# Sixteen more frames by gather in a hybrid encoder block with product-key experts

## The chip, the cores and the metric

The kernel runs on one NeuronCore of a Trainium2 chip. The metric is device time in microseconds of one execution. TensorE multiplies (its stationary operand is loaded by a separate instruction), VectorE and ScalarE do elementwise work, GpSimd (POOL) builds tiles and issues indirect transfers, SyncE (SP) issues plain ones; 16 DMA engines move the data.

## The reference

One layer over 512 frames of width 2048, in float32, and a final norm:

```
xn = rmsnorm(x);  p_rw, q, c_kv, iq, ik, iw, gates = split(xn @ w_in)
y_a = rwkv7(p_rw) @ w_branch_rwkv            # 16 heads of 64, a recurrence over time
y_b = dsa(q, c_kv, iq, ik, iw) @ w_branch_dsa # 16 heads; iq, ik, iw choose 256 keys per frame
h = x + (sig(gA) * y_a + sig(gB) * y_b) @ w_out
h2 = rmsnorm(h)
# product-key experts: 8 heads choose 16 of 16384 experts each, 128 per frame
out = h + sum_k gate_k * gelu(h2 . u[e_k]) * v[e_k]
return rmsnorm(out)
```

u and v are tables of 16384 rows of 2048 floats, 128 MB each.

## The kernel before

Every float32 matrix is split into a rounded high part and a remainder (`load_w`, L187; `split`, L224), and a product is three matmuls: high by high, high by low, low by high. `load_w` moves 512 KB into one of three `raw` buffers on SP's queue; ScalarE copies it to `whi` (L196), VectorE subtracts to `wlo` (L197), two buffers of each. `load_w` has a raised priority, so that it is placed ahead of about a hundred instructions. A planner orders the instructions of each engine before the run; each engine then works in that order.

Front: `r1` (L379) computes three small projection tiles and, for eight head pairs, three projection tiles and the pair's scaled tensors. `r1_pair` (L440) sums log decays by matmuls with the 256-column constant `u2`, which holds an inclusive and an exclusive lower triangle. `index` (L701) projects the latent keys, the index keys (tile 33, the 64 columns of `ik` twice: L735), the index queries and the queries, and interleaves the triangular `solve` on VectorE. `r2` runs the recurrence in chunks and projects the gates. `attention` (L863) evacuates V as [128, 4, 1024]; `head` (L895) multiplies 64 columns of V by the transposed weights into the upper or lower 64 rows of one PSUM tile (L922). `mix` and `peer` (L928) follow.

Experts: the 512 frames are treated in two ways. The last ND = 352 go through the dense loop, all 16384 experts for every frame, with gates that are zero for experts not chosen. The first NG = 160 gather their own 128 rows of u and of v.

`route` (L1026) computes the choice, writes one-hot gate products to DRAM (`d_g`, 22 groups of 16 frames: L1120 on) and, between, the activations of the first EARLY = 24 blocks of 128 experts (`early`, stored in `d_a`). `experts` (L1156) goes over 16 groups `cg` of eight blocks. For each block it takes the activation (`act`: two loads of 512 KB and 48 matmuls; or a copy from `d_a`), multiplies it by G, the group's gates (one buffer, read from `d_g`), and splits it into Wh and Wl (eight buffers each). Then 16 output blocks `db`: one load of 512 KB and 24 matmuls (L1195 to L1197) each, added to `accT` by VectorE (L1202). The order of groups is 3, 0, 4, 1, 5, 2, 6, ...: groups 0 to 2 are wholly early, the others not.

`gathered` (L988) is a generator of 320 steps, and `step` (L980) takes from it at an even rate as the dense loop proceeds, two units per computed block and one per `db`. A step is an indirect transfer of 128 rows of 8 KB into one of three `rows` buffers (issued by POOL) and one VectorE instruction over 2048 elements: a dot product with `ra`/`rb` (L1002) or an accumulation (L1011). Frames 128 to 159 use four partitions each (32 steps per table), frames 0 to 127 one (128 steps per table). `issue_after` places a step's VectorE instruction behind the last `wlo`.

At the last group the activations' pool is closed, `turned` (L1213) loads the residual and transposes `accT` block by block, and after `db` 11 the rest of the steps and `final_gathered` (L1247) are issued: load h into a buffer `hg` (one, for both blocks of frames), fold the four partitions by matmuls, add, square, norm, store. `final` norms and stores the dense frames.

```
        self.due += n * 320 / (512 - 2 * EARLY - 10)
...
        order = [g for i in range(n) for g in (n + i, i)] + list(range(2 * n, 16))
...
                if last and db == 11:
                    for _ in items:
                        pass
                    self.final_gathered()
```

Of the kernel before, what the change touches and what calls it, by code (L numbers as in the profile page):

```python
# [30 lines left out]
T = 512  # L31
# [6 lines left out]
NTILE = 74  # L38
NG = 160
ND = T - NG  # L40
EARLY = 24

VEC = {}
_o = 0
# [7 lines left out]
for _n, _w in (("ident", 128), ("iota", 128), ("onesbd", 128), ("ones64", 128), ("onesD", 2), ("onesR", 2), ("u2", 256),  # L52
               ("mtt", 128), ("mm1", 128), ("mbr", 64), ("m32", 128), ("c30", 128), ("c38", 128), ("fold", 128)):
    CON[_n] = (_o, _w)
    _o += _w
NCON, NKEEP = _o - 128, 256


def columns():
    r = np.arange  # L60
    none = lambda n: np.full(n, -1)
    tiles = [r(3072, 3200), r(3200, 3328), np.concatenate([r(3328, 3360), r(5216, 5224), none(88)])]
# [4 lines left out]
    tiles += [np.concatenate([r(5152, 5216)] * 2)]  # L67
# [6 lines left out]
def constants():  # L74
    c = np.zeros((128, NCON + 128), np.float32)
# [12 lines left out]
    put("u2", np.concatenate([(hp == hf) & (p <= f), (hp == hf) & (p < f)], 1))  # L88
# [7 lines left out]
    put("fold", p % 32 == f % 32)  # L96
# [69 lines left out]
class Kernel:  # L166
# [105 lines left out]
    def build(self):  # L272
        tc, nc = self.tc, self.nc
        with ExitStack() as es:
# [19 lines left out]
            self.d_iq = d("d_iq", [4, 2, 128, 512])  # L294
            self.d_ya = d("d_ya", [2, 8, 128, 512], F32R)
            self.d_gate = d("d_gate", [16, 128, 2, 512])
            self.d_h = d("d_h", [T, D])
            self.d_g = d("d_g", [ND // 16, 16, 128, 128])
            self.d_a = d("d_a", [EARLY, 128, ND])
# [79 lines left out]
    def r1(self, xs):  # L379

        nc, io = self.nc, self.io
        with ExitStack() as es:
# [10 lines left out]
            with self.pool("r1w") as wp:  # L393
# [20 lines left out]
                nc.scalar.activation(iwT[32:64], ps[32:64], AF.Copy, scale=IDX_SCALE)  # L414
                pw = self.wk()
# [24 lines left out]
    def r1_pair(self, p, z, sp, rp, zwa, wicl, lws):  # L440
# [5 lines left out]
        P, Pm, Pi = t1("P"), t1("Pm"), t1("Pi")  # L446
        for b in range(2):
            pc = self.wk()
            for u in range(2):
                nc.tensor.matmul(pc[:, 256 * u:256 * u + 256], lws[:, 2 * b + u, fs], self.c("u2"), start=True, stop=True)  # L450
            g = pc.rearrange("p (u e t) -> p u e t", u=2, e=2)
            o = lambda a: a[:, 256 * b:256 * b + 256].rearrange("p (u t) -> p u t", u=2)
            nc.scalar.activation(o(P), g[:, :, 0], AF.Exp, scale=-CDEC)
            nc.scalar.activation(o(Pm), g[:, :, 1], AF.Exp, scale=-CDEC)
            nc.scalar.activation(o(Pi), g[:, :, 0], AF.Exp, scale=CDEC)
# [16 lines left out]
        v.tensor_tensor(sp[:, 0], kk, Pm, op=ALU.mult)  # L472
# [56 lines left out]
    def r2(self, xs):  # L529
# [3 lines left out]
        with ExitStack() as es:  # L533
# [8 lines left out]
            for p in range(8):  # L542
# [14 lines left out]
                for m in (2 * p, 2 * p + 1):  # L557
                    for j in range(2):
                        ps = self.mm()
                        self.gemm(ps, io["w_in"][42 + 2 * m + j], xs)  # L560
# [140 lines left out]
    def index(self, xs, steps):  # L701
# [7 lines left out]
        with ExitStack() as es:  # L709
# [41 lines left out]
            for h in range(8):  # L751
                ps = self.mm()
                gemm(ps, io["w_in"][34 + h])
# [109 lines left out]
    def attention(self, es, ybh, ybl):  # L863
# [5 lines left out]
        V = kp.tile([128, 4, 1024], F32, name="Vh")  # L869
        for sb in range(4):  # L870
            for hf in range(2):
# [4 lines left out]
                sc.activation(V[:, sb, f], ps, AF.Copy)  # L876
# [18 lines left out]
    def head(self, h, qb, ap, B, qs, ks, V, ybh, ybl):  # L895
# [3 lines left out]
        s = slice(64 * (h % 2), 64 * (h % 2) + 64)  # L899
# [28 lines left out]
    def peer(self):  # L928
# [3 lines left out]
        with ExitStack() as es:  # L932
# [3 lines left out]
            self.ra = gk.tile([128, D], F32, tag="ra", name="ra")  # L936
            self.rb = gk.tile([128, D], F32, tag="rb", name="rb")
            for n, w, dt in (("eid", 128, I32), ("act", 128, F32), ("gate", 128, F32)):
                setattr(self, n + "a", gk.tile([128, w], dt, name=n + "a"))
                setattr(self, n + "b", gk.tile([128, w // 4], dt, name=n + "b"))  # L940
# [4 lines left out]
            with self.pool("hn") as np_:  # L945
# [18 lines left out]
                nc.gpsimd.tensor_tensor(self.rb[0:32], hn[0:32, 1], gf[0:32], op=ALU.mult)  # L964
                for j in range(1, 4):
                    nc.gpsimd.dma_start(self.rb[32 * j:32 * j + 32], self.rb[0:32])
                nc.gpsimd.tensor_tensor(self.ra, hn[:, 0], gf, op=ALU.mult)
# [12 lines left out]
    def step(self, items, n=1):  # L980

        self.due += n * 320 / (512 - 2 * EARLY - 10)
# [5 lines left out]
    def gathered(self):  # L988

        nc, io = self.nc, self.io  # L990
        v = nc.vector

        def rows(table, eid, s):
            r = self.rows.tile([128, D], F32, name="rows")
# [3 lines left out]
        for x, n in (("b", 32), ("a", 128)):  # L998
            h, eid, act, gate = [getattr(self, m + x) for m in ("r", "eid", "act", "gate")]
# [4 lines left out]
            nc.scalar.activation(act, act, AF.Gelu)  # L1004
            v.tensor_tensor(act, act, gate, op=ALU.mult)
            o = self.gk.tile([128, D], F32, tag="r" + x, name="o" + x)
            setattr(self, "r" + x, o)
            for s in range(n):
# [5 lines left out]
                yield  # L1014

# [10 lines left out]
    def route(self, es, xs):  # L1026
# [8 lines left out]
        eid1 = kp.tile([32, 128], I32, name="eid1")  # L1035
# [3 lines left out]
        with ExitStack() as es3:  # L1039
# [3 lines left out]
            for h in range(8):  # L1043
# [48 lines left out]
                for e, b in ((self.eida, 0), (eid1, 1)):  # L1092
# [201 lines left out]
```

## Time and profile before

| | us |
|---|---|
| runs shown | 4137.31, 4136.78, 4130.66 (median 4136.78) |
| profiled execution | 4133.32, span 4131.5 |
| TensorE busy | 3993.7 |
| VectorE busy | 2810.0 |
| ScalarE busy | 1413.8 |
| POOL busy | 797.0 |

The profile is of one execution, so sums are made against 4133.32. Engine names in rows: PE is TensorE (PEld its weight loads), DVE VectorE, ACT ScalarE, POOL GpSimd, SPq SyncE's queue. A busy TensorE is not one at its peak: the durations of its instructions overlap, so paces are read from starts. A row of a stretch has its bounds, its length, the busy time of PE, PEld, DVE, ACT and POOL (with their instructions), the granted clock as a share of 2.4 GHz, the DMA engines' busy share and GB/s. A row of a group has its instructions' busy time and the mean ns of one.

### The profile page before, as it was taken

The page shows a single profiled execution, that of the slowest core. Times are in us where ns is not written, and L with a number is a line of the kernel's source. Part 1 is how long each engine was busy: PE and PEld are TensorE (multiplying, and loading weights), DVE is VectorE, ACT ScalarE, POOL GpSimd, SP SyncE. Part 2 cuts the span into 40 slices and gives each one's busy share as a digit, 9 for nine tenths or more (in the row PEclk, how much of TensorE's full clock was granted, in tenths as well). Part 3 has the DMA queues.
Part 4 walks back from the last instruction along what each step waited for, and adds up shares of the span by engine and source line. Part 5 has one row for each costly group of instructions (what it writes and reads, how often), then busy time and mean ns, then how long its engine had stood idle before and what let it go on. Part 6 is the DMA issues. An engine that isn't in the chain of part 4 may idle for free.

```text
span 4131.5 us, 57533 instructions
## 1 busy us (share of the span) xinstructions
PE 3993.7 (97%) x22313; PEld 3599.7 (87%) x22313; DVE 2810.0 (68%) x4713; ACT 1413.8 (34%) x2079; POOL 797.0 (19%) x919
## 2 busy tenths in 40 slices
PE   8999999999999999999999999999999999999996
PEld 6777778888886788788899998989999999999996
DVE  5444589434434552389976778878888888888886
ACT  4222332223224422332486333323333333333332
POOL 2000211101003300100364222221222221222220
PEclk9999999999999999999999999999999999999998
DMA  4333852332226433333476888988989989999885
GB/s 147 121 127 128 186 177 85 99 101 91 86 93 192 141 133 138 128 130 110 158 214 207 332 318 323 332 323 325 335 332 344 337 328 332 343 342 340 330 332 175
DMA packets 254657, 910.36 MB, mean 220 GB/s; under 512 B 26912, under 2 KB 78240, under 8 KB 210384
## 3 DMA queue, kind: packets, MB, share of 16 engines
q1 hardware_dynamic: 132800, 447.21, 31.4%
q0 software_dynamic: 76176, 436.41, 29.6%
q10 hardware_dynamic: 45408, 23.07, 2.0%
q8 instruction: 175, 2.87, 0.3%
q14 instruction: 98, 0.80, 0.1%
HBM read 830.07 MB, written 75.66 MB: 219 GB/s over the span
## 4 chain that ended last, share of the span: by engine, by line
PE 57%; issue 12%; DMA 5%; POOL 3%; DVE 3%; ACT 2%; POOLq 0%; DVEq 0%; ACTq 0%; SPq 0%
PE mm L213 9%; PE mm L214 9%; PE mm L212 9%; PE wk L1197 5%; PE wk L1196 5%; PE wk L1195 5%; POOL rows L995 3%; PE wk L856 1%; PE wk L855 1%; PE wk L857 1%; PE po L212 1%; PE po L213 1%; DMA G<-d_g 1%; PE po L214 1%; PE po L922 1%
## 5 line engine op out<-in xcount | busy, mean ns | idle before, releaser
L196 ACT ACTIVATE whi<-raw 128x1024 fp32r<-128x1024 f32 x760 | 804.1, 1059 | 1955.9 <-PE mm L213 1018.1
L197 DVE TENSOR_TENSOR wlo<-raw,whi 128x1024 fp32r<-128x1024 f32 x760 | 934.1, 1230 | 773.5 <-ACT whi L196 710.4
L1197 PE MATMUL wk<-Wh,wlo 128*128 128x352 f32 x2048 | 668.5, 327 | 17.4 <-DVE wlo L197 17.3
L1195 PE MATMUL wk<-Wh,whi 128*128 128x352 f32 x2048 | 666.0, 327 | 15.2 <-ACT Wh L225 11.4
L1196 PE MATMUL wk<-Wl,whi 128*128 128x352 f32 x2048 | 669.0, 327 | 0.3 <-DVE Wl L226 0.2
L212 PE MATMUL mm<-h2h,whi 128*128 128x352 f32 (+1 forms) x1920 | 641.0, 334 | 5.2 <-ACT whi L196 5.0
L214 PE MATMUL mm<-h2h,wlo 128*128 128x352 f32 (+1 forms) x1920 | 640.8, 334 | 0.6 <-DVE wlo L197 0.6
L213 PE MATMUL mm<-h2l,whi 128*128 128x352 f32 (+1 forms) x1920 | 639.9, 333 | 0.0
L212 PE MATMUL mm<-xh,whi 128*128 128x512 f32 x1184 | 479.6, 405 | 6.6 <-DVE lo L715 5.1
L213 PE MATMUL mm<-xl,whi 128*128 128x512 f32 x1184 | 476.5, 403 | 0.6 <-POOL xl L344 0.5
L214 PE MATMUL mm<-xh,wlo 128*128 128x512 f32 x1184 | 474.0, 400 | 2.0 <-DVE wlo L197 2.0
L1197 PEld LDWEIGHTS wk<-Wh,wlo 128*128 128x128 f32 x2048 | 388.6, 190 | 25.4 <-DVE wlo L197 24.8
L1195 PEld LDWEIGHTS wk<-Wh,whi 128*128 128x128 f32 x2048 | 387.9, 190 | 22.0 <-ACT Wh L225 13.6
L1196 PEld LDWEIGHTS wk<-Wl,whi 128*128 128x128 f32 x2048 | 388.1, 190 | 3.9 <-DVE Wl L226 3.1
L212 PEld LDWEIGHTS mm<-h2h,whi 128*128 128x128 f32 x1920 | 362.3, 189 | 16.6 <-ACT whi L196 5.3
L214 PEld LDWEIGHTS mm<-h2h,wlo 128*128 128x128 f32 x1920 | 361.4, 188 | 13.0 <-DVE wlo L197 2.1
L213 PEld LDWEIGHTS mm<-h2l,whi 128*128 128x128 f32 x1920 | 363.2, 189 | 10.5
L1011 DVE SCALAR_TENSOR_TENSOR oa<-rows,acta,oa 128x2048 f32<-128x2048 f32 x127 | 297.8, 2345 | 3.0 <-DMA rows<-in_rv_dram,eida 2.9
L1002 DVE CUSTOM_DVE_ANT_0 rows<-rows,ra 128x2048 f32<-128x2048 f32 x128 | 292.1, 2284 | 2.9 <-DMA rows<-in_ru_dram,eida 2.9
L212 PEld LDWEIGHTS mm<-xh,whi 128*128 128x128 f32 x1184 | 224.6, 190 | 60.6 <-DVE lo L715 5.3
L213 PEld LDWEIGHTS mm<-xl,whi 128*128 128x128 f32 x1184 | 224.7, 190 | 56.4 <-issue 3.8
L214 PEld LDWEIGHTS mm<-xh,wlo 128*128 128x128 f32 x1184 | 224.3, 189 | 56.6 <-DVE wlo L197 2.4
(437 smaller groups left out, 5809.9 us busy)
## 6 DMA issues: line engine op xcount, KB each, us to landing
raw<-in_pu_dram SPq DMA_DIRECT2D x256, 512.0 KB, 5.9
raw<-in_pv_dram SPq DMA_DIRECT2D x256, 512.0 KB, 7.3
raw<-in_w_in_dram SPq DMA_DIRECT2D x148, 512.0 KB, 3.8
d_g<-Gs ACTq DMA_DIRECT2D x22, 1024.0 KB, 6.2
G<-d_g POOLq DMA_DIRECT2D x16, 1408.0 KB, 14.1
raw<-in_wbr_dram SPq DMA_DIRECT2D x32, 512.0 KB, 4.0
raw<-in_wout_dram SPq DMA_DIRECT2D x32, 512.0 KB, 3.5
raw<-in_wpq_dram SPq DMA_DIRECT2D x32, 512.0 KB, 3.6
```

The source lines that it names most:

```text
L196: nc.scalar.activation(hi, raw, AF.Copy)
L197: self.last = nc.vector.tensor_tensor(lo, raw, hi.bitcast(F32), op=ALU.subtract).ins
L212: nc.tensor.matmul(ps, hi[:, s], xh, start=k == 0, stop=False)
L213: nc.tensor.matmul(ps, hi[:, s], xl, start=False, stop=False)
L214: nc.tensor.matmul(ps, lo[:, s], xh, start=False, stop=k == nk - 1)
L855: mmul(ps[tb], yh[:, k, t], hi[:, s], start=k == 0, stop=False)
L995: nc.gpsimd.indirect_dma_start(out=r, out_offset=None, in_=table, in_offset=bass.IndirectOffsetOnAxis(ap=eid[:, s:s + 1], axis=0))
L1002: v.tensor_tensor_reduce(r, r, h, 1.0, 0.0, op0=ALU.mult, op1=ALU.add, accum_out=act[:, s:s + 1])
L1011: v.scalar_tensor_tensor(o, r, act[:, s:s + 1], o, op0=ALU.mult, op1=ALU.add)
L1195: mmul(ps, hi[:, s], wh, start=j == 0, stop=False)
L1196: mmul(ps, hi[:, s], wl, start=False, stop=False)
L1197: mmul(ps, lo[:, s], wh, start=False, stop=j == 7)
```

## The change

NG goes from 160 to 176, ND from 352 to 336. The gathered frames are three groups: 16 frames with eight partitions each (16 steps per table), 32 with four, 128 with one: 176 steps per table. Their normed inputs go to DRAM (`d_h2`) and are read back per group. Each group ends with its own fold, residual, norm and store inside `gathered`, in buffers of the `rows` ring, at four steps per group; `final_gathered` is gone, and the steps that remain are issued before the last group's output blocks.

24 early blocks remain, but two in each even group of eight and one in each odd one; the groups run in order 0 to 15. The rate of steps is now 364 over 256 + 2 x 104 - 20 units.

Two joined changes: `u2` holds the inclusive triangle alone, in 128 columns, and the exclusive factor is the inclusive one shifted by a column, with the first column of each 64-frame chunk copied; and V is kept as [64 columns, 64 zeros, 64 columns] per pair of heads, so that both heads of a pair accumulate over all 128 rows of the same PSUM tile.

The index keys' 64 columns move into the unused columns of projection tile 2; the split is stored to DRAM (`d_ik`) and read back in `index`. Tile 33 is gone.

```diff
-NTILE = 74
-NG = 160
+NTILE = 73
+NG = 176
-EARLY = 24
+GROUPS = ((160, 16, 8), (128, 32, 4), (0, 128, 1))
+EARLY = [8 * g + j for g in range(16) for j in range(2 - g % 2)]
...
+                ik = [wp.tile([128, T], F32R, name=f"ik{i}") for i in range(2)]
+                nc.scalar.activation(ik[0][64:128], ps[64:128], AF.Copy)
+                nc.vector.tensor_tensor(ik[1][64:128], ps[64:128], ik[0][64:128].bitcast(F32), op=ALU.subtract)
+                for i in range(2):
+                    nc.gpsimd.dma_start(self.d_ik[i], ik[i][64:128].bitcast(F32))
...
-                nc.tensor.matmul(pc[:, 256 * u:256 * u + 256], lws[:, 2 * b + u, fs], self.c("u2"), start=True, stop=True)
+            nc.tensor.matmul(pc[:, 128 * b:128 * b + 128], lws[:, b, fs], self.c("u2"), start=True, stop=True)
...
-        v.tensor_tensor(sp[:, 0], kk, Pm, op=ALU.mult)
+        v.tensor_tensor(sp[:, 0, 1:], kk[:, 1:], P[:, 0:T - 1], op=ALU.mult)
+        v.tensor_copy(sp[:, 0, 0:T:64], kk[:, 0:T:64])
...
-            ps = self.mm()
-            gemm(ps, io["w_in"][33])
-            sc.activation(ik, ps, AF.Copy)
-            v.tensor_tensor(ik[64:128], ps[64:128], ik[64:128].bitcast(F32), op=ALU.subtract)
+            for i in range(2):
+                nc.gpsimd.dma_start(ik[64 * i:64 * i + 64].bitcast(F32), self.d_ik[i])
...
-        V = kp.tile([128, 4, 1024], F32, name="Vh")
+        V = kp.tile([128, 4, 8, 192], F32, name="Vh")
+        nc.gpsimd.memset(V.rearrange("p s a d -> p (s a) d")[:, :, 64:128], 0.0)
...
-            mmul(self.po[s, 128 * qb:128 * qb + 128], V[:, j, 64 * h:64 * h + 64], PT[:, 128 * j:128 * j + 128],
-                 start=j == 0, stop=j == qb)
+            mmul(self.po[:, 128 * qb:128 * qb + 128], V[:, j, h // 2, s], PT[:, 128 * j:128 * j + 128],
+                 start=h % 2 == 0 and qb == 3 and j == 0, stop=h % 2 == 1 and qb == 0)
...
-        self.due += n * 320 / (512 - 2 * EARLY - 10)
+        self.due += n * self.rate
...
+        for i, (t0, m, parts) in enumerate(GROUPS):
+            eid, act, n = self.eid[i], self.act_[i], 128 // parts
+            h = row("h2t")
+            for j in range(parts):
+                nc.gpsimd.dma_start(h[m * j:m * j + m], self.d_h2[t0:t0 + m])
...
+            h, g = get(), get()
+            nc.gpsimd.dma_start(h[:m], self.d_h[t0:t0 + m])
+            nc.gpsimd.dma_start(g[:m], io["gfin"].to_broadcast([m, D]))
+            yield
+            if parts > 1:
+                for q in range(4):
+                    f = slice(512 * q, 512 * q + 512)
+                    ps = self.wk()
+                    nc.tensor.matmul(ps, self.fold[:, 128 * i:128 * i + 128], o[:, f], start=True, stop=True)
+                    v.tensor_tensor(h[:m, f], ps[:m], h[:m, f], op=ALU.add)
+            else:
+                v.tensor_tensor(h, o, h, op=ALU.add)
+            s = self.gk.tile([128, 1, 1], F32, name="ss0")
+            sc.activation(o[:m], h[:m], AF.Square, accum_out=s[:m, 0])
+            yield
+            yield
+            v.scalar_tensor_tensor(h[:m], h[:m], self.inverse(self.gk, s[:m]), g[:m], op0=ALU.mult, op1=ALU.mult)
+            nc.sync.dma_start(self.out[t0:t0 + m], h[:m])
+            yield
...
-        order = [g for i in range(n) for g in (n + i, i)] + list(range(2 * n, 16))
+        self.rate = sum(2 * (128 // g[2]) + 4 for g in GROUPS) / (256 + 2 * (128 - len(EARLY)) - 20)
...
-        for cg in order:
-            first, last = cg == order[0], cg == order[-1]
+        for cg in range(16):
+            first, last = cg == 0, cg == 15
...
-                if e < EARLY:
+                if e in EARLY:
...
             if last:
+                for _ in items:
+                    pass
                 self.left.close()
...
-                if last and db == 11:
-                    for _ in items:
-                        pass
-                    self.final_gathered()
```

## Rows read from the trace of the kernel before

**Rows 1.** The page: the span, and part 1, busy time of each engine.

```profile
span 4131.5 us, 57533 instructions
...
PE 3993.7 (97%) x22313; PEld 3599.7 (87%) x22313; DVE 2810.0 (68%) x4713; ACT 1413.8 (34%) x2079; POOL 797.0 (19%) x919
```

**Rows 2.** Busy time in two stretches of the expert loop; then the second, row buffers alone.

```profile
2290.00:2820.00 530.00, 505.06 (x3042) 495.75 (x3041) 423.25 (x437) 165.57 (x204) 115.76 (x96) 0.98 0.89 328
2820.00:4040.00 1220.00, 1212.30 (x7499) 1202.98 (x7498) 999.68 (x938) 398.63 (x473) 267.47 (x235) 1.00 0.91 335
...
2820.00:4040.00 1220.00, 506.64 (x220) 0.00 (x0) 251.38 (x219) 1.00 0.91 335
```

**Rows 3.** What TensorE waited for, 2290 to 2820 us: total, times, longest.

```profile
PE wk L1195 <- ACT Wh L225: 11.4, 6, 3.8
PE wk L1197 <- DVE wlo L197: 11.2, 6, 2.9
```

**Rows 4.** TensorE's timeline (start, duration): first and last of 27 and of 57 matmuls.

```profile
999.72 0.40 PE L212 MATMUL mm<-xh,whi 128*128 128x512 f32 x1
...
1005.81 0.39 PE L214 MATMUL mm<-xh,wlo 128*128 128x512 f32 x1
...
2999.70 0.32 PE L213 MATMUL mm<-h2l,whi 128*128 128x352 f32 x1
...
3008.72 0.32 PE L212 MATMUL mm<-h2h,whi 128*128 128x352 f32 x1
```

**Rows 5.** Groups of TensorE's instructions by line and shape.

```profile
L1195 PE MATMUL wk<-Wh,whi 128*128 128x352 f32 x2048 | 666.0, 327 | 15.2 <-ACT Wh L225 11.4 <-ACT whi L196 3.8
L212 PE MATMUL mm<-h2h,whi 128*128 128x352 f32 x1664 | 539.6, 324 | 5.0 <-ACT whi L196 5.0
...
L1137 PE MATMUL wk<-ob,oa 128*128 128x128 f32 x704 | 92.1, 278 | 6.3 <-ACT oa L1133 4.4 <-POOL oa L1130 1.9
...
L922 PE MATMUL po<-PT,Vh 128*64 128x128 f32 x320 | 50.8, 285 | 0.4
...
L450 PE MATMUL wk<-con,lws 128*128 128x256 f32 x64 | 15.1, 378 | 0.0
```

**Rows 6.** TensorE's timeline in the attention.

```profile
1297.52 1.09 PE L922 MATMUL po<-PT,Vh 128*64 128x128 f32 x8
1298.54 0.51 PE L906 MATMUL wk<-ks,twice 128*128 128x256 f32 x2
1298.97 0.87 PE L922 MATMUL po<-PT,Vh 128*64 128x128 f32 x6
1299.77 0.50 PE L214 MATMUL mm<-yah,wlo 128*128 128x512 f32 x1
```

**Rows 7.** Busy time in three short stretches (last columns: clock, DMA share, GB/s).

```profile
3600.00:3700.00 100.00, 98.96 (x613) 97.84 (x612) 83.54 (x72) 32.84 (x40) 22.95 (x20) 1.00 0.94 350
2500.00:2520.00 20.00, 17.67 (x104) 16.85 (x103) 14.61 (x14) 5.42 (x7) 5.80 (x4) 0.97 1.01 365
4040.00:4050.00 10.00, 6.48 (x32) 5.85 (x31) 6.64 (x11) 1.06 (x1) 0.00 (x0) 0.83 1.02 397
```

**Rows 8.** VectorE's timeline at the start of the expert loop.

```profile
2268.77 1.39 DVE L1178 TENSOR_TENSOR gel<-gel,G 128x352 f32<-128x352 f32 x3 [8.02 <-DMA raw<-in_pu_dram]
```

**Rows 9.** Timeline of the end.

```profile
4103.08 0.56 POOL L1253 DMA_DIRECT2D hg<-d_h  x1 [71.17 <-DMA out_dram<-hg]
...
4105.77 1.91 DVE L1244 TENSOR_TENSOR res<-res,gf 128x512 f32<-128x512 f32 x3 [0.65 <-ACT sqf L1243]
...
4117.25 0.16 DVE L252 TENSOR_SCALAR inv<-inv 128x3 f32<-128x3 f32 x1
...
4119.62 2.48 DVE L1277 TENSOR_SCALAR res<-res,rsr 128x2048 f32<-128x2048 f32 x2
```

**Rows 10.** The row buffers' tile, 2900 to 4000 us: waits before it (us, times), landing.

```profile
  DMA rows<-in_ru_dram,eida: 2.9, 3
...
DMA to landing us min/median/max: 5.3/8.9/17.2
```

More of the change, by code (lines that the diff above doesn't have):

```diff
@@ L875, in attention @@
                 self.latent(ps, [(self.cth[:, r, c], self.ctl[:, r, c]) for r in range(2)], [(wuv[r][0][:, f], wuv[r][1][:, f]) for r in range(2)])
-                sc.activation(V[:, sb, f], ps, AF.Copy)
+                for u in range(2):
+                    sc.activation(V[:, sb, 4 * hf:4 * hf + 4, 128 * u:128 * u + 64],
+                                  ps.rearrange("p (a u d) -> p u a d", a=4, u=2)[:, u], AF.Copy)
         units = []
@@ L935, in peer @@
             gk = self.gk = E(self.pool("gk"))
[L936 to L940, printed above, removed]
+            self.eid, self.act_, self.gate = [[gk.tile([128, 128 // g[2]], dt, name=f"{n}{i}") for i, g in enumerate(GROUPS)]
+                                              for n, dt in (("eid", I32), ("act", F32), ("gate", F32))]
+            self.fold = gk.tile([128, 256], F32, name="fold")
+            nc.gpsimd.dma_start(self.fold, io["con"][:, NCON:])
             self.left = ExitStack()
@@ L990, in gathered @@
         nc, io = self.nc, self.io
-        v = nc.vector
+        v, sc = nc.vector, nc.scalar
+        row = lambda name: self.gk.tile([128, D], F32, tag="r", name=name, bufs=2)
+        get = lambda: self.rows.tile([128, D], F32, name="rows")
         def rows(table, eid, s):
-            r = self.rows.tile([128, D], F32, name="rows")
+            r = get()
             nc.gpsimd.indirect_dma_start(out=r, out_offset=None, in_=table,
@@ L1003, in gathered @@
                 yield
[L1004 to L1007, printed above, removed]
+            sc.activation(act, act, AF.Gelu)
+            v.tensor_tensor(act, act, self.gate[i], op=ALU.mult)
+            o = row("out")
             for s in range(n):
@@ L1091, in route @@
                     next(early, None)
-                for e, b in ((self.eida, 0), (eid1, 1)):
+                for e, b in ((self.eid[-1], 0), (eid1, 1)):
                     m = e.shape[0]
@@ L1245, in turned @@
             yield
-    def final_gathered(self):
-        nc = self.nc
-        v, sc = nc.vector, nc.scalar
-        for x, t0, m in (("b", 128, 32), ("a", 0, 128)):
-            h = self.fp.tile([128, D], F32, name="hg")
-            nc.gpsimd.dma_start(h[:m], self.d_h[t0:t0 + m])
-            o = getattr(self, "r" + x)
-            if x == "b":
-                for q in range(4):
-                    f = slice(512 * q, 512 * q + 512)
-                    ps = self.wk()
-                    nc.tensor.matmul(ps, self.fold, o[:, f], start=True, stop=True)
-                    v.tensor_tensor(h[:m, f], ps[:m], h[:m, f], op=ALU.add)
-            else:
-                v.tensor_tensor(h, o, h, op=ALU.add)
-            s = self.fp.tile([128, 1, 1], F32, name="ss0")
-            j = self.rows.tile([128, D], F32, name="rows")
-            sc.activation(j[:m], h[:m], AF.Square, accum_out=s[:m, 0])
-            v.scalar_tensor_tensor(h[:m], h[:m], self.inverse(self.fp, s[:m]), self.gf[:m], op0=ALU.mult, op1=ALU.mult)
-            nc.sync.dma_start(self.out[t0:t0 + m], h[:m])
     def final(self):
```

76 lines of the change are left out of this document (35 added, 41 removed).

## The prediction

> **What bounds the kernel now.** I read the page's totals first: TensorE is busy 97% of a 4131.5 us span, the next engine (VectorE) 68% [rows 1]. A share of the whole span hides stages, so I then took the expert loop by itself, in long windows. From 2820 to 4040 us TensorE is busy 1212.30 of 1220 us, VectorE 82% (999.68), and the 16 DMA engines 0.91 at 335 GB/s [rows 2]. The reader is to see that TensorE sets the time, with two others close behind it. From 2290 to 2820 us TensorE lacks 25 us, and the view of what it waited for names the cause: 11.4 us for Wh, 11.2 us for wlo [rows 3]. These are the groups whose eight experts were all computed ahead: TensorE has nothing to do until VectorE and ScalarE have weighted eight activations.
>
> Next I needed the price of a column. In the timeline of TensorE 27 matmuls of 512 columns start between 999.72 and 1005.81 us, so 6.09/26 = 234.2 ns each; 57 of 352 columns between 2999.70 and 3008.72 us, so 9.02/56 = 161.1 ns each [rows 4]. Both are 0.4575 ns per column with nothing left over, at a granted clock of 1.00 (its level of 2.4 GHz). The durations of single rows overlap, so starts are what counts.
>
> Durations below come from the profiled execution: span 4131.5 us, 4133.32 us with what lies around it. The median shown, 4136.78 us, is 3.5 us more; I sum against 4133.3 and add 3.5 at the end. A difference under 0.2% (8 us) can't be told from none.
>
> **The change part by part.** I call 24 matmuls on one 512 KB load a unit: an expert's activation is two units, one of the 256 output blocks one.
>
> *336 dense columns instead of 352.* 16 fewer columns are 7.32 ns per matmul. The expert loop holds 104 x 48 + 256 x 24 = 11,136 of them (the groups of 1664 and 2048 rows, three lines each, [rows 5]): -81.5 us. The 24 early experts add 1152: -8.4 us. One of 22 one-hot groups goes: 16 matmuls in two passes each, about 0.1 us a pass, -3.2 us. A unit falls from 3.87 to 3.69 us.
>
> *One projection tile less.* 16 x 3 matmuls of 512 columns at 234.2 ns: -11.2 us. The two small copies move to the tile before and have TensorE work over them; four POOL transfers of 128 KB stay behind others and I cost them at nothing (1 us if they delay a load).
>
> *Prefix sums of 128 columns instead of 256.* 64 passes [rows 5]. A 256-column pass is busy 378 ns, a 128-column one 278: 0.1 us each, -6.4 us.
>
> *Full-width attention outputs.* Eight passes with 64 weight columns take 1.02 us from their start to the next instruction's, six take 0.80 [rows 6]: 0.11 us a pass plus 0.14 us per run, and the weight load goes in with a gap each way. There are 64 such runs. Full-width passes cost the same (278 against 285 ns busy [rows 5]), and I expect the fixed part to go: -9 us, between 0 (the gap has another cause) and -15. The zeroing of V and eight more ScalarE copies run before the first use; at most +3.
>
> *Early experts spread, two or one per group.* No group is left without activations to compute, so the 25 us of [rows 3] go, and with them the half-clock stretches behind each gap (0.97 granted over one such window of 20 us [rows 7]): -28 us, between -18 and -35. Late next is the loop's start: VectorE weights the first activations by G only at 2268.77 us, after 8.02 us of idling, three at once [rows 8] (the weight load named there doesn't feed this instruction; G does). Before, the first group computed eight activations, and three of them waited for G then. Now the first two are copies that need no TensorE, in a ring of three: TensorE has less to do until G lands. +5 us, between 0 and two activations (15).
>
> *Norm of gathered frames inside the gather.* Now the 128-frame block is loaded at 4103.08 us, after 71.17 us in which its single buffer waited for the 32-frame block's store; its sum, square and norm then stand ahead of the last scaling at 4119.62 us [rows 9]. VectorE is done with the dense rows at 4105.77 + 1.91 = 4107.7; with its own chain of small steps (eleven of them in the 2.37 us from 4117.25) the scaling could start at 4110.1: -9.5 us, between -6 and -12. The moved work (per block two full-width steps of some 2.3 us [rows 2] and the small ones, about 7 us of VectorE; three blocks, their loads on POOL, three stores on SP) comes into the gather. Each store waits on VectorE with the weight loads of SP queued behind it, and each block takes two of the three row buffers, so that fewer gathers are in flight for some 10 us; one more set of four folding matmuls waits for the last accumulation. +6 us, between 0 and +25.
>
> *32 more gathers.* VectorE: 219 gather steps in these 1220 us cost 506.64 us, 2.31 each [rows 2]. All steps now spread over 444 of 464 units, 364 steps of which 352 gather: 0.79 per unit instead of 219/316 = 0.69. VectorE per unit: 999.68/316 = 3.16, plus 0.10 x 2.31, less 0.02 for narrower operands, plus 0.05 for the norms: 3.42 of 3.69 us, 93%. It stays under TensorE, but with 0.27 us to spare instead of 0.70.
>
> DMA, per unit: 0.524 MB of weights, 0.79 x 1.049 = 0.83 of rows, 0.05 of G, some 0.025 of copies, 1.43 MB. At TensorE's pace that is 1.43/3.69 = 388 GB/s, against 335 now. What can the engines give? At a share of 0.94 they moved 350, so 372 at 1.0; where the share is 1.01 over 20 us they moved 365, and 397 where it is 1.02 over 10 us [rows 7]. Their mean is 378; I take 376, as bursts flatter. So 444 x 1.43 = 635 MB take 1690 us and TensorE's units 1638: overload +50 us, between 0 (at 388 or more) and +102 (at 365). This is the step I know least.
>
> The Trainium skill speaks against it: its page DMA: Bandwidth & Descriptors (section Where 436 GB/s comes from) says that for transfers between HBM and SBUF the HBM side binds, at about 358 GB/s per core. By it the overload would be 635/358 - 1638 = 136 us. The windows of 365 and 397 lie above it; the HBM Reference (section Specifications) says that a core streaming alone is well above the share of a pair.
>
> Sum: -81.5 -8.4 -3.2 -11.2 -6.4 -9 -28 +5 -9.5 +6 +50 = -96.2; 4133.3 - 96.2 + 3.5 = 4040.6.
>
> **The rivals.**
> A: the overload is hidden. The row ring and the weight ring smooth it, and full engines give 390 or more. For it: the window at 397, and that VectorE waited only 2.9 us for rows in 1100 us [rows 10]. Against: 20-us windows at full share gave 365. 4041 - 50 = 3991 us.
> B: the engines hold no more than about 360 GB/s over a whole loop, between the 350 that they held over 100 us and the 365 of a full 20-us window. 635 MB then take 1764 us, overload 126: 4041 + 76 = 4117 us, barely faster. Against: shares near 1 came only in bursts so far, and the rate rose with the share each time [rows 7]. The Trainium skill's rule of 358 above is this case, with 4127 us.
> C, slower: the ring of three row buffers becomes the bound. A buffer's round is POOL's issue (251.38/219 = 1.15 us), VectorE's step (2.31 [rows 2]) and the landing, 8.9 us in the median and up to 17.2 [rows 10]; three buffers give one row set per 4.1 us at best, and 3.69/0.79 = 4.65 are wanted. Without the overload term all others sum to -146, so the change stops paying when the gathers take 1638 + 146 = 1784 us, 5.07 each: a landing of 11.7 us, a third more than now. At 12.5 us it is 352 x 5.32 = 1873, overload 235, 4226 us. For it: landings lengthen when engines are full, and VectorE, in order, holds wlo behind a late row set. Against: today each round has some 16 us for 12 us of work.
> D: weight loads set the pace, and fewer columns buy nothing. For it: they are busy 99% of the loop [rows 2]. Against: eight passes, each with a load, fit in 1.02 us [rows 6], and the pace is proportional to columns. Then -81.5 goes and so does the overload, 4073 us.
>
> **How the numbers follow.** Forecast (4005 to 4085 us) 0.59; A 0.19; B 0.13; C 0.06; D 0.03. Predicted is the likeliest, 4041. The low end takes A in, 3985; the high end reaches toward B to 4105, and leaves out C, most of B and a little below A, under 0.2. B's centre is 20 us under the median, and its upper part (to 4150) lies beyond 8 us under it: 0.03 of its 0.13 counts as the same, 0.01 as slower; with C that makes slower 0.06 + 0.01 = 0.07, same 0.03, faster 0.90.
>
> **What would show it.** Dense matmuls 0.154 us apart in undisturbed stretches (D wrong). No idle bursts in the first groups; the first G step with a gap as now or somewhat longer. DMA share at 0.97 or more and 370 to 380 GB/s until some 75 us before the last matmul, TensorE below 98% there; at 385 and 99% it is A, at 360 B. Row landings of 10 us and VectorE waiting for rows tens of us in all; at 12 us C. The last scaling some 5 us after the last dense sum. The prediction is wrong in kind if the loop's loss comes from the start or from the three norms instead of from transfers.

## The result

The changed kernel takes 4102.56 us (median of five runs, 4092.73 to 4112.05), the kernel before 4136.36 on the same chip: ratio 0.9921, 95% interval 0.9905 to 0.9937. That is 34 us faster, where 96 were forecast; the time lies inside the range, near its upper end. The profiled execution took 4096.14 us, its span 4094.4.

The page after: the span, and part 1, busy time of each engine.

```profile
span 4094.4 us, 57543 instructions
...
PE 3903.1 (95%) x22241; PEld 3511.4 (86%) x22241; DVE 2861.5 (70%) x4766; ACT 1393.1 (34%) x2044; POOL 958.7 (23%) x980
```

TensorE has 91 us less to do than before [rows 1], and the span is only 37 us shorter: 54 us came back as idle time. The two stretches of the expert loop that answer to [rows 2]:

```profile
2280.00:2800.00 520.00, 494.42 (x3067) 479.76 (x3067) 432.02 (x437) 166.86 (x206) 158.28 (x109) 0.98 0.93 343
2800.00:3960.00 1160.00, 1103.37 (x6973) 1083.85 (x6972) 1010.22 (x967) 365.57 (x437) 363.48 (x248) 0.98 0.95 362
```

The first is 95% busy as it was; the second, the undisturbed loop, fell from 99% to 95%. VectorE is at 87% there, the DMA engines at 0.95 and 362 GB/s. What TensorE waited for from 2200 to 4100 us (total, times, longest), against [rows 3], and then VectorE's waits on transfers:

```profile
PE wk L1231 <- DVE wlo L199: 57.0, 42, 6.2
PE mm L214 <- ACT gel L1181: 10.9, 2, 8.9
...
PE wk L1229 <- ACT Wh L227: 5.0, 10, 1.3
```

```profile
DVE rows L1015 <- DMA rows<-in_ru_dram,eid: 44.4, 28, 6.3
...
DVE out L1023 <- DMA rows<-in_rv_dram,eid: 20.0, 21, 2.9
DVE gel L1210 <- DMA G<-d_g: 18.4, 5, 5.0
```

TensorE waits for wlo, which VectorE makes; VectorE stands before it in order, for rows (64 us, 34 of them from 2900 to 4000 us, where [rows 10] had 2.9) or for G. One such chain, on VectorE and then on TensorE:

```profile
2875.08 2.29 DVE L1015 CUSTOM_DVE_ANT_0 rows<-rows,h2t 128x2048 f32<-128x2048 f32 x1 [4.38 <-DMA rows<-in_ru_dram,eid]
2877.29 0.08 DVE L1015 DVE_READ_ACCUMULATOR2_ANT act<- 128x1 f32 x1
2877.29 1.22 DVE L199 TENSOR_TENSOR wlo<-raw,whi 128x1024 fp32r<-128x1024 f32 x1
```

```profile
2878.57 0.42 PE L1231 MATMUL wk<-Wh,wlo 128*128 128x336 f32 x1 [2.85 <-DVE wlo L199]
```

A row set lands 4.38 us late, the split behind it is late, TensorE idles 2.85 us.

By place: the last one-hot matmul comes 31 us earlier (2245.7 to 2214.4 us; forecast -11.2 -6.4 -9 -3.2 -8.4 = -38); the tail behind the last dense matmul went from 28.3 to 18.4 us (-9.9; forecast -9.5); the stretch between went from 1857.6 to 1861.7 us, +4 where -81.5 -28 +5 +6 +50 = -48 were forecast. So 52 us of the miss lie in the loop and 7 in front of it.

### The profile page after: what moved, and what is told of

It reads as the page before. It is cut to its first block, busy times and chain, and to the rows that moved or that the text cites. A ratio compares the mean times of both kernels' runs of the same rounds, so it can differ in the third digit from the quotient of the medians.

```text
span 4094.4 us, 57543 instructions
## 1 busy us (share of the span) xinstructions
PE 3903.1 (95%) x22241; PEld 3511.4 (86%) x22241; DVE 2861.5 (70%) x4766; ACT 1393.1 (34%) x2044; POOL 958.7 (23%) x980
## 3 DMA queue, kind: packets, MB, share of 16 engines
q0 software_dynamic: 82144, 474.71, 31.3%
## 5 line engine op out<-in xcount | busy, mean ns | idle before, releaser
L1231 PE MATMUL wk<-Wh,wlo 128*128 128x336 f32 x2048 | 658.6, 323 | 57.2 <-DVE wlo L199 57.0
L1229 PE MATMUL wk<-Wh,whi 128*128 128x336 f32 x2048 | 660.4, 323 | 16.1 <-ACT whi L198 10.9
L1230 PE MATMUL wk<-Wl,whi 128*128 128x336 f32 x2048 | 657.1, 321 | 2.3 <-DVE Wl L228 2.2
L214 PE MATMUL mm<-h2h,whi 128*128 128x336 f32 (+1 forms) x1920 | 630.6, 328 | 12.8 <-ACT gel L1181 10.9
L216 PE MATMUL mm<-h2h,wlo 128*128 128x336 f32 (+1 forms) x1920 | 630.8, 329 | 8.5 <-DVE wlo L199 8.2
L215 PE MATMUL mm<-h2l,whi 128*128 128x336 f32 (+1 forms) x1920 | 629.6, 328 | 0.0
L1015 DVE CUSTOM_DVE_ANT_0 rows<-rows,h2t 128x2048 f32<-128x2048 f32 x176 | 401.7, 2284 | 44.6 <-DMA rows<-in_ru_dram,eid 44.4
L1023 DVE SCALAR_TENSOR_TENSOR out<-rows,act,out 128x2048 f32<-128x2048 f32 x173 | 405.7, 2345 | 20.8 <-DMA rows<-in_rv_dram,eid 20.0
L1005 POOL DMA_INDIRECT rows<-in_ru_dram,eid x176 | 263.9, 1500 | 595.2 <-DVE act L1015 540.7
L1005 POOL DMA_INDIRECT rows<-in_rv_dram,eid x176 | 258.8, 1470 | 600.1 <-DVE out L1023 531.2
L214 PEld LDWEIGHTS mm<-h2h,whi 128*128 128x128 f32 x1920 | 363.6, 189 | 24.1 <-ACT gel L1181 11.4
```

The lines of the kernel that those rows point to most:

```text
L214: nc.tensor.matmul(ps, hi[:, s], xh, start=k == 0, stop=False)
L215: nc.tensor.matmul(ps, hi[:, s], xl, start=False, stop=False)
L216: nc.tensor.matmul(ps, lo[:, s], xh, start=False, stop=k == nk - 1)
L1005: nc.gpsimd.indirect_dma_start(out=r, out_offset=None, in_=table, in_offset=bass.IndirectOffsetOnAxis(ap=eid[:, s:s + 1], axis=0))
L1015: v.tensor_tensor_reduce(r, r, h, 1.0, 0.0, op0=ALU.mult, op1=ALU.add, accum_out=act[:, s:s + 1])
L1023: v.scalar_tensor_tensor(o, r, act[:, s:s + 1], o, op0=ALU.mult, op1=ALU.add)
```

## The experiments

Each was run against the kernel before in three rounds; a ratio without a kernel named is to the kernel before. "After" is the changed kernel.

**VectorE's work or the transfers.** Halved transfers: each gather brings 1024 of the 2048 floats, VectorE reads them twice. Halved VectorE work: whole rows arrive, VectorE computes on half of each.

```diff
-indirect_dma_start(out=r, in_=table, ...)
+indirect_dma_start(out=r[:, 0:1024], in_=table.rearrange("a (b f) -> (a b) f", b=2), ...)   # halfdma
...
-v.scalar_tensor_tensor(o, r, act, o, ...)
+v.scalar_tensor_tensor(o[:, 0:1024], r[:, 0:1024], act, o[:, 0:1024], ...)                    # halfdve
```

> The changed kernel with each gather fetching 128 half rows (4 KB instead of 8 KB; VectorE reads the half twice, so its instructions keep their 2048 elements; the expert outputs of the gathered frames are not the reference's). Bytes (the DMA engines' rate is what the loop lost to): 185 MB less, TensorE back to its own pace, waits in the loop from some 95 us to under 30, about 4025 us. Row ring (three buffers, landing time): landings shrink too, same direction, 4025 to 4050. VectorE (in order, 93% loaded): its work stays, under 15 us gained, 4090.

> The changed kernel with VectorE's gather steps over 1024 instead of 2048 columns (half of the work of the gathered frames' experts left out), the transfers unchanged. Bytes: at most 15 us faster, 4090. Row ring: a buffer's round is 1.1 of some 13 us shorter, 4075 to 4090. VectorE: its load falls from 86% to about 65%, 40 to 60 us faster, 4045 to 4060.

Half the bytes: 4012.09 us, ratio 0.9698 (0.9682 to 0.9715), 90 us faster than after. Half VectorE's steps: 4095.97, 0.9900 (0.9884 to 0.9917), 7 to 9 us less by medians and ratios, with intervals that overlap. The loop with half the bytes, and then with half of VectorE's steps:

```profile
2800.00:3960.00 1160.00, 1137.41 (x7303) 1122.54 (x7302) 1039.13 (x1016) 388.71 (x466) 368.55 (x252) 1.00 0.78 265
```

```profile
2800.00:3960.00 1160.00, 1104.09 (x6981) 1087.49 (x6980) 776.71 (x964) 366.84 (x438) 275.89 (x248) 0.98 0.96 362
```

With half the bytes TensorE is back at 98%, and VectorE at 90%, higher than in after. With half of VectorE's steps that engine is at 67%, the transfers as full as in after, and TensorE gains nothing. So VectorE's load is at most a small part of the cause; what the bytes bring with them is the large one, at 90 us instead of the 50 forecast.

**The ring of row buffers.** A fourth buffer, a fifth (with two gel buffers, which hold activations, instead of three, to make room), and a fourth in the kernel before.

```diff
+self.rows2 = R(self.pool("rows2", 1, side="right"))
-get = lambda: self.rows.tile([128, D], F32, name="rows")
+def get():
+    self.turn4 += 1
+    return (self.rows if self.turn4 % 4 else self.rows2).tile([128, D], F32, name="rows")
```

> The changed kernel with four row buffers instead of three. Bytes: within 10 us of 4102, since the engines move the same. Row ring: the round may last a third longer, VectorE's 63 us of waiting for rows mostly go, 4040 to 4065. VectorE: within 15 us, 4090 to 4102.

> Five row buffers instead of three (a ring of gel of two instead of three makes room). Three gave 4102.6, four 4070.2, with VectorE's waits for rows down from 64 to 22 us and the transfers up from 354 to 360 GB/s between 2240 and 3960 us. If the ring is what keeps the DMA engines from being busy all the time, a fifth buffer gives some 10 to 20 us more: 4050 to 4060, 365 GB/s. If four buffers reached the limit of the engines, 4064 to 4074. The shorter gel ring costs up to 8 us at the loop's start.

> The kernel before with four row buffers: a control. There VectorE waited 2.9 us for rows in 1100 us, with the engines at a share of 0.89. If the ring costs time only where transfers and TensorE are both near their limits, no difference: within 6 us of 4136. If a fourth buffer is worth 30 us in any case (four buffers gain by something that has nothing to do with the change), 4100 to 4115.

Four buffers: 4070.23 us, 0.9849 (0.9832 to 0.9865). Five: 4075.27, 0.9863 (0.9845 to 0.9880), nothing more in sum; but the shorter ring of gel is in it (TensorE's longest wait for gel, at the loop's start, is 24.1 us against 14.1 with four), so a fifth buffer by itself was not measured. The kernel before with four: 4125.71, 0.9980 (0.9970 to 0.9990), 8 us. First after, then four buffers over 1720 us of the loop:

```profile
2240.00:3960.00 1720.00, 1635.78 (x10278) 1600.78 (x10278) 1473.07 (x1435) 546.17 (x661) 534.52 (x367) 0.98 0.94 356
```

```profile
3200.00:3300.00 100.00, 99.05 (x642) 98.19 (x641) 89.61 (x99) 33.53 (x41) 31.57 (x22) 1.00 0.98 383
2240.00:3960.00 1720.00, 1650.49 (x10469) 1612.60 (x10468) 1496.10 (x1459) 557.25 (x676) 536.96 (x370) 0.99 0.95 360
```

VectorE's waits for rows fall from 64 to 22 us, and 14.9 of these are one wait at the start. So about 30 of the 90 us were the ring's, four times what a fourth buffer is worth in the kernel before; with a fifth the mean rate is the same (also 360 GB/s). The forecast's figure for full engines, 376 GB/s at a share of 1, holds: 356/0.94 = 379, and 383 over the 100 us shown. What doesn't hold is the share of 1.

**The 16 frames alone.** All other edits, with 160 gathered frames.

```diff
-NG = 176
-GROUPS = ((160, 16, 8), (128, 32, 4), (0, 128, 1))
+NG = 160
+GROUPS = ((128, 32, 4), (0, 128, 1))
```

> The changed kernel with 160 gathered frames as before (groups of 32 frames in four partitions and 128 in one) and all the other edits. Bytes: demand per unit is back at some 340 GB/s and the waits at before's 25 us without the first groups' 25; 4136 less the front's 20, the route's and start's few, the 25 and the end's 9.5: about 4075, faster than with 176. Row ring: the same. VectorE: the same direction. If instead 16 more frames do pay, it lies above 4102, at 4110 to 4130.

4119.68 us, 0.9967 (0.9953 to 0.9982). So the 16 frames pay 17 to 19 us, where -81.5 -8.4 -3.2 +50 = -43 were forecast, and the other edits together 14 to 16, where the forecast gives them 53. Both halves fell short.

**The spread of the early experts.** Undone in three kernels: after, the one with 160 frames, the one with half the bytes.

```diff
-EARLY = [8 * g + j for g in range(16) for j in range(2 - g % 2)]
+EARLY = list(range(24))
...
-for cg in range(16):
+for cg in [3, 0, 4, 1, 5, 2] + list(range(6, 16)):
```

> The changed kernel with the spread alone undone: the 24 early experts are the whole of groups 0 to 2 again, and the groups run in the order of the kernel before (3, 0, 4, 1, 5, 2, 6 to 15). The forecast priced the spread at -28 us (stalls on Wh and wlo 25, half clock 3) and +5 at the start: undone, the time should rise by 18 to 30, to 4121 to 4133. The theory that the spread only moves its stall to the group boundaries and the start: within 8 us of 4102. If bytes set the loop: within 5 us as well, as a group without activations has fewer loads just there and lets the rings fill.

> The kernel with 160 gathered frames and all other edits (4119.7 us), with the spread alone undone: here transfers are at 340 GB/s, further from their limit than with 176 frames, so the spread shows its own price. By the forecast it is worth 23 us: 4143 us without it. By the theory that it only exchanges three stalls for sixteen waits on G: 4115 to 4125. If transfers hide it with 176 frames only: 4135 or more here, against the 7 us that undoing it cost there.

> Gathers of half the bytes (the gathered frames' results are not the reference's) and the spread undone: 24 early experts fill groups 0 to 2 again. With half the bytes alone the time was 4012.1, so transfers don't hide here what the spread is worth. By the forecast it is worth 23 us: 4035. If it only exchanges one set of stalls for another: 4005 to 4020.

4109.40 us, 0.9933 (0.9912 to 0.9954), against 0.9921 with the spread; 4113.88, 0.9944 (0.9928 to 0.9961), against 0.9967; 4022.68, 0.9714 (0.9696 to 0.9732), against 0.9698. By medians and ratios the spread is worth 5 to 11 us in the first and the third, where the intervals overlap, and costs 6 to 10 in the second; nowhere does it give 23. Why is seen in the time from one group's first output matmul to the next's, read from TensorE's timeline (medians, the loop's start left out; "units" is units times 24 matmuls at the measured pace):

| us | units | before | 160 frames | after | four buffers | half the bytes |
|---|---|---|---|---|---|---|
| none early | 32 x 3.87 = 123.8 | 125 | | | | |
| next wholly early | 16 x 3.87 = 61.9 | 67 | | | | |
| behind a wholly early one | 123.8 | 132 | | | | |
| next has one early | 30 units | | 120 (116.1) | 118 (110.4) | 117 | 114 |
| next has two early | 28 units | | 114 (108.4) | 113 (103.0) | 110 | 108 |

Before, three pairs of groups lost 13 us each (5 + 8) and the others one; with the spread every group loses 4 to 6 even where transfers don't bind. In after each loses 8 to 10, in all groups alike. The columns differ in more than the spread; for like with like, from the first output matmul to the last the kernel with 160 frames takes 1827.0 us for 452 units, with the spread undone 1812.8 for 448: 79 and 81 us above the units' pace, the same loss in other places. With half the bytes it is 73 and 87.

**Waits on G.** The early activation needs no computing, so its multiply by G comes up as soon as G has landed. In the kernel with 160 frames, POOL, then VectorE, then TensorE:

```profile
2871.76 1.41 POOL L1200 DMA_DIRECT2D G<-d_g  x1
```

```profile
2870.86 0.52 DVE L1210 TENSOR_TENSOR gel<-gel,G 128x352 f32<-128x352 f32 x1
...
2887.81 0.52 DVE L1210 TENSOR_TENSOR gel<-gel,G 128x352 f32<-128x352 f32 x1 [6.01 <-DMA G<-d_g]
2888.26 1.22 DVE L199 TENSOR_TENSOR wlo<-raw,whi 128x1024 fp32r<-128x1024 f32 x1
```

```profile
2889.53 0.58 PE L1231 MATMUL wk<-Wh,wlo 128*128 128x352 f32 x1 [4.24 <-DVE wlo L199]
```

G has one buffer, so it is loaded only when the group's last multiply is done (2870.86), and lands 16 us later with the next multiply already at the head of VectorE's queue, in the middle of the output blocks. Edits that should take this away, each by itself:

```diff
+                if db == 4 and not last: nextG = load_G(cg + 1)                              # gahead
-EARLY = [... for j in range(2 - g % 2)]
+EARLY = [... for j in range(6 + g % 2, 8)]                                                   # lastearly
-G = dp.tile([128, ng, 8, 16], F32, name="G")
+G = dp.tile([128, ng, 8, 16], F32, name="G", bufs=2)                                         # gtwo, ng160g2
-v.tensor_tensor(a3, a3, G[:, :, j], op=ALU.mult)
+with self.tc.issue_after(self.last) if e in EARLY else ExitStack():                          # r4gaft, halfgaft
+    v.tensor_tensor(a3, a3, G[:, :, j], op=ALU.mult)
```

> The changed kernel with one move: the G of the next group is issued after the fifth output block of the group before, not at the group's start, so that it lands some 40 us before its first use. Theory 1 (VectorE stands in order behind the first G multiply of each group, because the early block's activation is ready at once while G is still landing): the stalls on G after the first group go (13.5 us of VectorE in the loop after 2100 us, part of it the start), and TensorE's dips at the group boundaries with them; 5 to 15 us faster than the changed kernel's 4102.6, that is 4088 to 4098. Theory 2 (bytes at the engines' full rate set the loop, and a stall of VectorE is made up later): no difference, within 4 us of 4102. Theory 3 (the ring of row buffers): no difference either.

> The changed kernel with the two early experts (one in odd groups) last in each group instead of first, so that G is first needed after a computed activation of 7.4 us, and the loop starts with TensorE at work. Theory 1 (stall on G at VectorE's head): the loop start's wait of 9 to 14 us shrinks to nothing and the group boundaries close: 15 to 30 us faster, 4073 to 4088. Theory 2 (bytes): 0 to 5 us faster, 4097 to 4103, since the same 635 MB pass. Theory 3 (row ring): the same as theory 2. A cost against it: the last two activations leave TensorE only VectorE's weighting of them to wait for at the start of the output blocks.

> The changed kernel (4102.6 us) with two buffers for G. Issuing G some blocks earlier in the program left its place in POOL's queue and the waits on it as they were, because the single buffer is free only after the group's last multiply. VectorE waits on G for 18.4 us in 5 waits here. Theory 1 (these waits reach TensorE): 8 to 15 us faster, 4088 to 4095. Theory 2 (transfers set the pace, a wait of VectorE is time that the row buffers use to fill): within 5 us of 4102.6.

> The kernel with 160 gathered frames and all other edits of the change (4119.7 us), with two buffers for G. Its trace shows why: the single G is loaded only when the last multiply of a group is done (issue at 2871.76 us), lands 16 us later, and the next group's early activation, which needs no computing, has its G multiply standing in VectorE's queue by then (6.01 us of idling before 2887.81 us, TensorE then 4.24 us without wlo); 58.5 us of VectorE in 12 waits in all. Theory 1 (the spread turned the stalls at three groups into one at each group, through G): with G a group ahead these waits go, 15 to 25 us faster, 4095 to 4105. Theory 2 (transfers at their limit already at 160 frames): no more than 5 us faster, as the same bytes pass.

> Gathers of half the bytes (the gathered frames' results are not the reference's) with the G multiply of the early activations queued behind the split of the latest weights. 4012.1 without it. If VectorE's waits on G (19 us in 5 here, TensorE's waits on wlo 21 us) are part of the 21 us by which half the bytes missed the forecast without transfers (3991): 4000 to 4007. If VectorE makes them up: 4009 to 4015.

The first tells nothing of G: 4104.08 us, 0.9920, and in its trace G is issued at 2386.85 us where after has 2388.77; its buffer is free no earlier. It stands as a repeat of after. Early experts last: 4116.62, 0.9945 (0.9927 to 0.9964), 10 to 14 slower; the wait took another place:

```profile
PE wk L1230 <- DVE Wl L228: 38.7, 15, 7.5
PE wk L1229 <- ACT Wh L227: 23.4, 12, 4.0
```

The output blocks now stand for the weighting of copies that come late (VectorE waits 51.4 us for them). Two buffers for G: 4090.51, 0.9891 (0.9874 to 0.9907), 12 faster; with 160 frames 4114.95, 0.9945 (0.9929 to 0.9962), 5 us by the medians and 9 by the ratios, less than the 15 to 25 expected: VectorE's 58.5 us of waits on G became 38.9 us of waits for the copies (in an execution of 4131.72 us, the slowest of its four). In after the second buffer left VectorE's waits for G and the copies as long as they were (18.4 us on G; then 10.3 on G and 13.2 on copies), so by which wait it gains its 12 us is not shown. Half the bytes with the multiply queued later: 4007.02, 0.9679 (0.9663 to 0.9695), 5 to 8 us. So edits to the stalls on G are worth 5 to 12 us, not the whole miss.

**Start, norms, and both repairs together.** No early expert in the first group (with four buffers); the gathered frames' norms left out; four buffers with the early experts last, and with the later multiply.

```diff
-EARLY = [8 * g + j for g in range(16) for j in range(2 - g % 2)]
+EARLY = [8 * g + j for g in range(1, 16) for j in range(1 + (g < 10))]                       # r4start
...
-sc.activation(o[:m], h[:m], AF.Square, accum_out=s[:m, 0])
-v.scalar_tensor_tensor(h[:m], h[:m], self.inverse(self.gk, s[:m]), g[:m], ...)              # nonorm, with the load of g
```

> Four row buffers (4070.2) and no early expert in the first group (two in groups 1 to 9, one in 10 to 15, 24 as before), so that the loop starts with eight activations to compute. In the trace with four buffers TensorE waits 14.1 us there for a gel that waits for G. If that wait and the half clock behind it are a loss of their own: 4052 to 4062. If the start is bound by G's landing and VectorE in any order: 4066 to 4074.

> The changed kernel with the norms of the gathered frames left out: no square, no inverse, no scaling, no load of gfin, so those frames leave unscaled. The forecast gave the norms +6 us, between 0 and 25. By it: 4096. If the norms are the loop's loss (what would have made the forecast wrong in kind): 4060 to 4080, and the dips of the transfer rate at 2300 to 2400 and 2700 to 2800 us (306 and 312 GB/s) go. If transfers in the undisturbed stretches are the loss: 4093 to 4103, dips mostly gone, and the rest as it was.

> Four row buffers instead of three and the early experts last in each group: both repairs in one. Four buffers alone gave 4070. If the ring and the stall on G are two separate losses, they add: 4070 - (15 to 30) = 4040 to 4055. If the early experts' place matters only as far as a late row set holds VectorE, 4065 to 4072. If bytes at the full rate (367 GB/s in the run with four buffers) are what is left, 4060 to 4070.

> Four row buffers (4070.2) and the G multiply of the early activations queued behind the split of the latest weights, so that VectorE doesn't stand for G in the middle of the output blocks. Two buffers for G gave 12 us with three row buffers. If the waits on G (35.5 us of VectorE with four buffers) reach TensorE: 4050 to 4062. If they are only time in which rows land: within 4 us of 4070.

Start: 4069.53, 0.9853 (0.9833 to 0.9873), the same as with four buffers, although TensorE's wait of 16.1 us for gel is gone; its waits for wlo rose from 40.0 to 49.4. Norms left out: 4091.02, 0.9898 (0.9879 to 0.9917), 10 to 12 us, and the undisturbed loop as it was. Four buffers with early experts last: 4117.02, 0.9947 (0.9930 to 0.9963): the later weighting costs 41 to 47 us there, against 10 to 14 with three buffers. Four buffers with the later multiply: **4062.25 us, 0.9829** (0.9811 to 0.9847), the fastest of those that leave nothing out; it beats both kernels, by 71 us and by 40. VectorE's waits on G fell from 35.5 us in six to one of 11.6 at the start, TensorE's for wlo from 40.0 to 31.3, about the 8 us gained.

## Why the prediction was right in sign and wrong in size

*Fixed terms: right.* TensorE's timeline, first and last of 41 matmuls in a row, against [rows 4]:

```profile
3049.86 0.32 PE L216 MATMUL mm<-h2h,wlo 128*128 128x336 f32 x1
...
3055.99 0.32 PE L214 MATMUL mm<-h2h,whi 128*128 128x336 f32 x1
```

6.13/40 = 153.3 ns, 7.8 less than before (7.32 forecast, which is 5 us more over the loop), and rival D is out. The prefix sums gave -6.9 us (forecast -6.4), the projection tile -10.4 (-11.2), the one-hot groups with the early activations -12.9 (-11.6). The attention gave -6 (-9): eight full-width passes take 0.88 us and four 0.44, so 0.11 a pass and no fixed part, as argued from [rows 6]. Another 5 us were lost, 2.4 in the recurrence and 2.3 between the output projection and the first one-hot matmul; the cause of both stays open.

```profile
1267.76 1.13 PE L931 MATMUL po<-PT,Vh 128*128 128x128 f32 x8
1268.64 0.36 PE L915 MATMUL wk<-ks,twice 128*128 128x256 f32 x1
1268.85 0.61 PE L931 MATMUL po<-PT,Vh 128*128 128x128 f32 x4
1269.29 0.41 PE L924 MATMUL wk<-con,P 128*128 128x128 f32 x2
```

*The tail: right.* -9.9 for -9.5. The last scaling starts 2.5 us after the last dense sum [rows 9]:

```profile
4078.63 1.91 DVE L1272 TENSOR_TENSOR res<-res,gf 128x512 f32<-128x512 f32 x3 [0.66 <-ACT sqf L1271]
...
4083.02 2.48 DVE L1283 TENSOR_SCALAR res<-res,rsr 128x2048 f32<-128x2048 f32 x2
```

*32 more gathers, overload +50: the step that failed most.* It is the term "I take 376 ... 635 MB take 1690 us and TensorE's units 1638: overload +50". The rate at full engines was right and the rule was wrong: it lets the slower of two streams run without a pause and hides the other under it. The two are within about 3% of each other, tied by three buffers and by VectorE's order, and neither ran through: the engines' share stayed at 0.94 and TensorE at 95%. Measured by halving the bytes: 90 us. Some 30 of it is the ring, shown by the fourth buffer; the other 60 is near the 50 forecast, and is shown only as what halving the bytes gives beyond that. "VectorE stays under TensorE" was right.

The forecast's demand is a mean over all units, and the loss is not even within a group. One group of after, the first 30 us of its output blocks, then the rest up to the next group's:

```profile
2852.00:2882.00 30.00, 24.25 (x142) 22.87 (x141) 23.03 (x25) 7.18 (x8) 10.08 (x8) 0.95 0.99 366
2882.00:2966.00 84.00, 82.78 (x539) 82.50 (x538) 75.05 (x84) 27.99 (x34) 27.37 (x18) 1.00 0.93 356
```

First the engines are full and TensorE is at 81%, then TensorE is at 99% and the engines are at 0.93. From 2240 to 4080 us, 68 of TensorE's 85 us of idling and 44 of VectorE's 63 us of waits for rows lie in the 30 us behind an issue of G, in a quarter of the time. G is 1.4 MB (128 x 21 x 8 x 16 floats), in POOL's queue between the gathers. Whether its load, the copies or the start of the output blocks makes the peak, no run tells: two buffers for G left the load where it was.

Rival B had the mean rate: 360 GB/s over a whole loop, where 356 to 362 were measured, and its 4117 us is nearer than 4041. By the sign that the prediction named ("at 360 B") the run is B's. As a limit of the engines it did not hold, since they moved 383 over 100 us; the mean stayed low because they were not always busy. Rival C had the ring as its mechanism, but needed a landing of 11.7 us; in runs of after with one edit (two buffers for G, no norms) the median was 9.3, against 8.9 in [rows 10], and landings over 12 us were about as frequent (32 and 42 of 343, against 31 of 302). What shrank was the room: three buffers leave 3 x 4.65 = 14 us a round, and 9.3 of landing, 2.3 of VectorE and 1.5 of POOL's issue are 13.1 on the average, where the kernel before had 16 for 12. C took the median landing, and so put at nothing what a late landing costs when the room is 1 us; this reading is argued, the ring's 30 us are measured.

The Trainium skill's page DMA: Bandwidth & Descriptors (section Where 436 GB/s comes from) gives about 358 GB/s per core between HBM and SBUF. The loop's mean of 356 to 360 looks like it, but 383 over 100 us with four buffers, and that 356 came at a share of only 0.94, say that here it was no ceiling.

*The spread, -28 and +5: wrong.* "No group is left without activations to compute, so the 25 us go." They went and came back as 4 to 6 us in each of 15 groups, in part through G with its single buffer and through the copies. Here the spread is worth 5 to 11 us, not 23. The forecast priced "late next" only at the loop's start, which looks as forecast: a wait of VectorE for G, TensorE idle for 8.91 us, and over the 20 us around it a mean granted clock of 0.76, between its levels of 1.2 and 2.4 GHz. First VectorE, answering to [rows 8], then TensorE, then the window:

```profile
2231.54 1.35 DVE L1210 TENSOR_TENSOR gel<-gel,G 128x336 f32<-128x336 f32 x3 [7.13 <-DMA raw<-in_pu_dram]
```

```profile
2234.80 0.65 PE L214 MATMUL mm<-h2h,whi 128*128 128x336 f32 x1 [8.91 <-ACT gel L1181]
```

```profile
2220.00:2240.00 20.00, 11.09 (x56) 10.81 (x55) 9.39 (x15) 4.96 (x9) 2.53 (x2) 0.76 0.43 128
```

*Norms, +6: 10 to 12*, inside the bounds. The tail gained 9.9 us by giving them up, so moving them brought nothing in sum.

The loop's miss of 52 us: transfers +40, spread +16, norms +5, columns -5, 56 in all; with the 7 in front 63, and 4041 + 63 = 4104 for 4102.6. Terms that are removed one at a time need not add, and the start with four buffers shows one that didn't; the agreement is no proof of each size. The sign that the prediction named for "wrong in kind" did not come: the loss lies in the undisturbed loop, group after group, not in the start or the norms. Of the 60 us beyond the ring, what keeps the engines from a full share with four or five buffers (SP's weight loads with three raw buffers, VectorE's order, or the uneven demand within a group) was not told apart.

## What to carry to other kernels

Where a change brings a second resource within a few per cent of the first, don't price the result as the larger of two sums: take the share that the busiest of them has reached over a whole loop (0.94 here, not 1), compare the demands stage by stage and not by their means, and look at what couples them, the buffers and the engine that works in order. A stall that is spread out is not gone: ask of each edit that makes an operand ready early which other operand (here G, with one buffer) the engine will then wait for, and how often.

## What the runs showed of the hardware

With the engines nearly full (after, 2240 to 3960 us), the 44,190 packets of 8 KB on the gathers' queue took 0.331 us each in the mean on a DMA engine, the 54,528 packets of 4 KB on the weights' queue 0.180: 24.8 and 22.8 GB/s per engine. And 100 us at 383 GB/s and a share of 0.98 were reached with TensorE at 99%, so the two don't exclude each other; it is the mean that stays below. An issue of a gather on POOL took 1.68 us in the median in after, and 0.94 where VectorE's steps on the rows were halved; why was not followed up.
